# Reordering the head of a one-core decoder layer: x and its norm first, the modulation loads behind the w_in loads

## The chip, the cores and the metric

The kernel runs on one NeuronCore of a Trainium2 chip. The metric is the device time of one execution in microseconds (us), as the median of three runs. Matrix products run on the tensor engine (PE, with its weight loads as PEld), elementwise work on the vector engine (DVE), the scalar engine (ACT) and GpSimd (POOL). SyncE (SP) issues nearly all transfers from HBM; its queue and ACT's are shown as SPq and ACTq.

## The reference

One decoder layer on x (256 tokens, 1024 features). What matters here is how the first projection gets its input:

```python
c_act = jax.nn.silu(c)
mod = (c_act @ w_ada[l] + b_ada[l])[:, None, :]            # 1024 -> 6 x 1024
sh1, sc1, g1, sh2, sc2, g2 = jnp.split(mod, 6, axis=-1)
u = modulate(rmsnorm(h, norm1[l]), sh1, sc1)               # h = x; x_hat * (1 + sc1) + sh1
h = h + g1 * token_mixer(u, w_in[l], ...)                  # u @ w_in, retention, latent attention, w_out
u = modulate(rmsnorm(h, norm2[l]), sh2, sc2)
h = h + g2 * hier_moe(u, ...)                              # 32 experts, about 100 MB of weights
return rmsnorm(h, final_norm)
```

sh1 and sc1 need the first 2048 columns of w_ada (8 MB); every product u @ w_in needs them for its slice of features.

## The kernel before

All weights are streamed. SBUF is cut into 27 slots of 1 MB; a class `Loads` keeps a list of loads in a fixed order and issues each on SP's queue when a slot is free by a plan that a first pass over the program recorded. Accurate products are made of three: an operand is split into hi and lo parts (`split`: ACT writes hi at L463, DVE writes lo at L464), and hi x hi, lo x hi, hi x lo are summed (`mm3` at L378 to L380 for tokens on the partitions, `feat_mm` at L530 to L532 for features on the partitions).

The head of the kernel is a loop over k, eight slices of 128 features of u. For each slice it needs

- `ada` k: the 128 shift and 128 scale columns of w_ada for slice k, 1 MB, loaded as two transfers whose contiguous pieces are 128 columns (512 bytes). `ada_mm(k)` multiplies them with silu(c) on PE (L424) and DVE copies the sums out (L427). `mod_of(k)` turns them on PE (L440), and DVE makes the scale and shift columns `acl` and `shc` (L442 to L445).
- `x_turned(k)`: the normed x, turned by PE into a PSUM bank (L433).
- `u_of(k)`: ACT applies scale and shift from the PSUM bank (L449), ACT writes hi (L451), DVE lo (L452).
- `e0` k and `e1` k: the rows of w_in of slice k for 704 and for 512 columns (352 KB and 256 KB), split into three pieces. The two halves of `e0` feed twelve products of 352 columns (two groups of six, `n = 0, 1`), `e1` feeds twelve of 256 columns.

SP's order is ada 0, x, then for each k: ada k+1, e0 k, e1 k. After them come the other columns of w_in (the first is called rq1), rotary tables, and so on. PE's order in the loop is written out by hand: for 0 < k < 7 it is x_turned(k+1), ada_mm(k+1), the six products of n = 0, the turns of mod_of(k+1), the six of n = 1, then the twelve on `e1`. Until the first six products are issued the orders of DVE and ACT are written out as well; later a scheduler orders them. `keep_warm(n)` issues n products of ones on PE that no result uses (L387): nine at the start and eight after ada_mm(0).

In the start x arrives behind ada 0. ACT (L498) and DVE (L499) square it, POOL takes the power -1/2 (L368), ACT and DVE scale x (L511, L509), and PE turns the first slice.

Behind the last `u_of` ACT issues five small loads of its own (L1050 to L1054, router weights and biases); they are tied to come after the last L449. Then ACT copies the first finished sums out (L372) and splits rq1.

Of the kernel before, what the change touches and what calls it, by code (L numbers as in the profile page):

```python
# [9 lines left out]
F32 = mybir.dt.float32  # L10
# [3 lines left out]
AF = mybir.ActivationFunctionType  # L14
ALU = mybir.AluOpType
# [26 lines left out]
ATT_STEPS = ("s0",), ("s1",), ("t0",), ("o0", "t1", "s2"), ("o1", "s3"), ("t2",), ("o2", "t3"), ("o3",)  # L42
RET_STEPS = ("s0",), ("s1", "v0"), ("s2", "v1"), ("t0", "s3", "v2"), ("t1", "v3"), ("t2",), ("t3",)

WARM0 = 9, 8
WARM2 = 2
WARM3 = 1
WARM4 = 0
# [8 lines left out]
C_ID, C_IOTA, C_END = 0, 128, 160  # L57
# [147 lines left out]
def body(ctx, tc, A, out, plan=None):  # L205
    nc = tc.nc
    T, V, S, G, Q = nc.tensor, nc.vector, nc.scalar, nc.gpsimd, nc.sync
    st = ctx.enter_context(tc.tile_pool(name="st", bufs=1))
# [4 lines left out]
    LD = Loads(SL, plan)  # L213
    ring = Ring(SL)

    def bank(name="bank"):
        return PB.alloc(name)

    w_ada = A["w_ada"][0].rearrange("(k p) n -> p k n", p=128)
    w_in = A["w_in"][0].rearrange("(k p) n -> p k n", p=128)  # L220


    cst = st.tile([128, C_END], F32, name="cst")
    ev_s = SL.alloc("ev")
    csb = ev_s.t[:, 1024:1280].rearrange("p (k m) -> p k m", k=8)
    rows = ev_s.t[0:40, 1280:1408]
    x_s = SL.alloc("x")
    x = x_s.t.rearrange("p (b n) -> p b n", b=2)
# [8 lines left out]
    def ld_ada_early(k):  # L237
        def fn(t):
            v = t.rearrange("p (k s n) -> p k s n", k=8, s=2)
            for s in range(2):  # L240
                Q.dma_start(v[:, :, s, :], w_ada[:, :, s * 1024 + k * 128:s * 1024 + (k + 1) * 128])  # L241
        return fn

    def ld(view, src):
        def fn(t):
            n = 1
            for d in src.shape[1:]:
                n *= d
            Q.dma_start(t[:, :n].rearrange(view[0], **view[1]) if view else t[:, :n], src)  # L249
        return fn  # L250

    def ld_k(src):

        return ld(("p (k n) -> p k n", dict(k=src.shape[1])), src)


    LD.add(("ada", 0), ld_ada_early(0))
    LD.issue()
    for b in range(2):
        Q.dma_start(x[:, b, :], A["x"][0, b * 128:(b + 1) * 128, :])  # L260
    row_load(8, "norm1")
    row_load(16, "b_ada", 0, 2048)
    row_load(32, "q_norm")
    row_load(35, "kv_norm")
    for k in range(8):
        if k < 7:
            LD.add(("ada", k + 1), ld_ada_early(k + 1))
        LD.add(("e0", k), ld_k(w_in[:, k:k + 1, 4096:4800]))
        LD.add(("e1", k), ld_k(w_in[:, k:k + 1, 0:512]))
    uq = A["w_uq"][0].rearrange("(k p) n -> p k n", p=128)  # L270
    ukv = A["w_ukv"][0].rearrange("(k p) n -> p k n", p=128)
    def sq(name):
        return A[name][0].rearrange("(k p) n -> p k n", p=128)
# [5 lines left out]
    i = 0  # L279
    for name, c0 in (("rq1", 512), ("rk0", 1024), ("rk1", 1536), ("rv0", 2048), ("rv1", 2560), ("rg0", 3072), ("rg1", 3584),  # L280
                     ("gr0", 4800), ("gr1", 5312), ("gm0", 5824), ("gm1", 6336), ("w_mla_o", 0), ("w_mla_o", 512),
                     ("w_ret_o", 0), ("w_ret_o", 512)):
        for half in range(2):
            src = sq(name) if name in A else w_in
# [55 lines left out]
    ident = cst[:, C_ID:C_ID + 128]  # L340
# [15 lines left out]
    def small(n):  # L356
        if sml_n[0] + n > 256:
            sml_n[0] = 0
        a = sml[:, sml_n[0]:sml_n[0] + n]
        sml_n[0] += n  # L360
        return a
# [8 lines left out]
    def copy(eng, o, i):  # L370
        if eng is S:
            S.activation(o, i, AF.Copy)  # L372
        else:
            V.tensor_copy(o, i)
# [7 lines left out]
    def keep_warm(n, after=None):  # L382

        pb = bank()
        with tc.issue_after(after) if after is not None else ExitStack():
            for _ in range(n):
                T.matmul(pb.t, onesb, oneb[:, 0:1].to_broadcast([128, 512]), start=True, stop=True)  # L387
        pb.free()

    keep_warm(WARM0[0])  # L390

    u_s = SL.alloc("u")
    uf = u_s.t.rearrange("p (k t) -> p k t", k=8)
# [3 lines left out]
    xh = xh_s.t.rearrange("p (b n) -> p b n", b=2)  # L397
# [18 lines left out]
    shc = st.tile([128, 8], F32, name="shc")  # L416
    acl = st.tile([128, 8], F32, name="acl")

    def ada_mm(k, pa):

        ev = ev_s.t[:, 256 * (k % 2):256 * (k % 2 + 1)]
        t = LD.get(("ada", k)).t.rearrange("p (k n) -> p k n", k=8)
        for j in range(8):
            i = T.matmul(pa.t[32 * (j % 4):32 * (j % 4) + 32, :256], csb[:, j, :], t[:, j, :], start=j < 4, stop=j >= 4,  # L424
                         skip_group_check=True, tile_position=(0, 32 * (j % 4)))
        LD.done(("ada", k))
        V.tensor_copy(ev, pa.t[:, :256])  # L427
        return ev, i.ins

    def x_turned(k):  # L430
        px = bank()
        for b in range(2):
            T.transpose(px.t[:, b * 128:(b + 1) * 128], xh[:, b, k * 128:(k + 1) * 128], ident)  # L433
        return px

    last_u = [None]

    def mod_of(k, pa, ev):
        for i in range(2):
            T.transpose(pa.t[:, 256 + i * 128:256 + (i + 1) * 128], ev[:, i * 128:(i + 1) * 128], ident)  # L440
        sc = small(2)
        V.tensor_reduce(sc, pa.t[:, 256:512].rearrange("p (i j r) -> p i j r", i=2, j=4)[:, :, :, 0], AX.X, ALU.add)  # L442
        V.scalar_tensor_tensor(acl[:, k:k + 1], sc[:, 1:2], bsc1[:, k:k + 1], colt[:, 8 + k:9 + k], op0=ALU.add,
                               op1=ALU.mult)
        V.tensor_add(shc[:, k:k + 1], sc[:, 0:1], colt[:, 16 + k:17 + k])  # L445
        pa.free()

    def u_of(k, px):
        last_u[0] = S.activation(uf[:, k, :], px.t[:, 0:256], AF.Identity, bias=shc[:, k:k + 1], scale=acl[:, k:k + 1]).ins  # L449
        hi, lo = hi_lo("u", k)  # L450
        S.activation(hi, uf[:, k, :], AF.Copy)  # L451
        V.tensor_tensor(lo, uf[:, k, :], hi, ALU.subtract)  # L452
        px.free()

    u_blk = blk_of("u")

# [17 lines left out]
    colt = st.tile([128, 40], F32, name="colt")  # L474
    cs = st.tile([128, 8], F32, name="cs")
    G.memset(csb, 0.0)
    pb = bank()
    T.transpose(pb.t[:, :8], rows[:8, :], cst[:8, C_ID:C_ID + 8])
    th = small(8)
    S.activation(th, pb.t[:, 0:8], AF.Tanh, scale=0.5)  # L480
    V.tensor_scalar(th, th, 0.5, 0.5, op0=ALU.mult, op1=ALU.add)
    V.tensor_mul(cs, th, pb.t[:, 0:8])
    V.tensor_copy(csb[:, :, 0], cs)
    pb.free()
    pb = bank()
    T.transpose(pb.t[:, :37], rows[:37, :], cst[:37, C_ID:C_ID + 37])
    V.tensor_copy(colt[:, 8:37], pb.t[:, 8:37])
    pb.free()
    bsc1 = st.tile([128, 8], F32, name="bsc1")
    V.tensor_scalar(bsc1, colt[:, 24:32], 1.0, None, op0=ALU.add)  # L490
    pa0 = bank()
    ev0, i = ada_mm(0, pa0)
    keep_warm(WARM0[1])


    ss = small(4).rearrange("p (b h) -> p b h", b=2)
# [4 lines left out]
    rst = small(2)  # L501
    V.tensor_reduce(rst, ss, AX.X, ALU.add)
    rsqrt(rst, rst, 1.0 / D, EPS)
    mod_of(0, pa0, ev0)


    def scaled(b, c0, c1):
        if b:
            V.tensor_scalar(xh[:, 1, c0:c1], x[:, 1, c0:c1], rst[:, 1:2], None, op0=ALU.mult)  # L509
        else:  # L510
            S.activation(xh[:, 0, c0:c1], x[:, 0, c0:c1], AF.Copy, scale=rst[:, 0:1])  # L511

    scaled(0, 0, 128)
    scaled(1, 0, 128)
    scaled(0, 128, 384)
    scaled(1, 128, 1024)
    u_of(0, x_turned(0))
    hl0 = [split(early_w(0)[0], 352)]
    pa = bank()
    ev = ada_mm(1, pa)[0]  # L520
    keep_warm(WARM4)
    hl0.append(split(early_w(0)[1], 352))
    scaled(0, 384, 1024)
    def feat_mm(accs, hi, lo, mh, ml, k):

        for h in range(2):
# [9 lines left out]
    for k in range(8):  # L536
        hl = hl0 if k == 0 else []
        for w in early_w(k)[len(hl):]:
            hl.append(split(w, 352))
        LD.done(("e0", k))  # L540
        hl.append(split(LD.get(("e1", k)).t[:, :512].rearrange("p (k n) -> p k n", k=1), 512))
        LD.done(("e1", k))

        if 0 < k < 7:
            px, pa = x_turned(k + 1), bank()
            ev = ada_mm(k + 1, pa)[0]
        for n in range(2):
            s, hi, lo = hl[n]
            for b in range(2):
                mm3(eacc[n][b].t[:, :352], u_blk(k, b), (hi[:, 0, :], lo[:, 0, :]), k == 0, k == 7)  # L550
            s.free()
            if (n, k) == (0, 0):
                start.close()
                early = ExitStack()
                early.enter_context(tc.manual_schedule(engines={T.engine}))
                px = x_turned(1)
            if n == (k == 0) and k < 7:
                mod_of(k + 1, pa, ev)
                u_of(k + 1, px)
        if k == 0:  # L560
            eacc.append([bank("acc") for _ in range(2)])
        s, hi, lo = hl[2]
        feat_mm(eacc[2], hi[:, 0, :], lo[:, 0, :], *hi_lo("u", k), k)
        s.free()
    early.close()
    LD.margin = MARGIN[1]
    u_s.free()
# [981 lines left out]
    with tc.If(many > CAP):  # L1549
# [7 lines left out]
        for k2 in range(4):  # L1557
            pb = bank()
# [3 lines left out]
            for kk in range(2):  # L1562
                k = 2 * k2 + kk
                S.activation(u2[:, k, :], pb.t[:, kk * 256:(kk + 1) * 256], AF.Identity, bias=s2c[:, k:k + 1],
                             scale=a2c[:, k:k + 1])
# [4 lines left out]
        with tc.For_i(0, 32, 1) as e:  # L1570
            for n in ("w1", "w3", "w2"):
                src = A[n][0].rearrange("g i (p k) n -> (g i) p k n", p=128)
# [12 lines left out]
            for b in range(2):  # L1585
                for n in range(2):
                    pb = bank()
# [124 lines left out]
```

## Time and profile before

| | us |
|---|---|
| median of 3 runs (lowest to highest) | 521.34 (520.93 to 521.62) |
| the profiled execution | 521.56 |
| its span, first to last instruction | 519.8 |
| PE busy in the span | 492.7 (95%) |
| DVE, ACT, POOL busy | 286.4, 197.9, 56.8 |
| HBM read, mean rate over the span | 173.22 MB, 335 GB/s |

Times in the views are counted from the start of the span. Busy time of PE is modelled from its issue and says little of how dense it is; what releases an instruction, and when, is read from the views of waits and of instructions in order of time.

### The profile page before, as it was taken

The page shows a single profiled execution, that of the slowest core. Times are in us where ns is not written, and L with a number is a line of the kernel's source. Part 1 is how long each engine was busy: PE and PEld are TensorE (multiplying, and loading weights), DVE is VectorE, ACT ScalarE, POOL GpSimd, SP SyncE. Part 2 cuts the span into 40 slices and gives each one's busy share as a digit, 9 for nine tenths or more (in the row PEclk, how much of TensorE's full clock was granted, in tenths as well). Part 3 has the DMA queues.
Part 4 walks back from the last instruction along what each step waited for, and adds up shares of the span by engine and source line. Part 5 has one row for each costly group of instructions (what it writes and reads, how often), then busy time and mean ns, then how long its engine had stood idle before and what let it go on. Part 6 is the DMA issues. An engine that isn't in the chain of part 4 may idle for free.

```text
span 519.8 us, 8582 instructions
## 1 busy us (share of the span) xinstructions
PE 492.7 (95%) x3440; PEld 339.1 (65%) x3443; DVE 286.4 (55%) x525; ACT 197.9 (38%) x366; POOL 56.8 (11%) x50
## 2 busy tenths in 40 slices
PE   6899999999999999999999999999999989898994
PEld 2678999997887878888688887443344343434432
DVE  3455789884696987979966746414031313131213
ACT  3545773454677544557434424202020211121013
POOL 1000321411000001119800000000000000000000
PEclk9999999999999999999999999999999999999999
DMA  9999899788876782998689888999999999999992
GB/s 272 323 320 361 297 353 398 289 321 312 333 242 244 247 321 81 338 396 308 234 342 352 311 352 301 417 386 422 420 417 419 421 415 419 421 419 416 392 325 99
DMA packets 68097, 174.85 MB, mean 336 GB/s; under 512 B 5422, under 2 KB 27091, under 8 KB 57816
## 3 DMA queue, kind: packets, MB, share of 16 engines
q1 hardware_dynamic: 65602, 174.01, 89.8%
q10 hardware_dynamic: 2454, 0.27, 0.4%
q8 instruction: 28, 0.46, 0.4%
q14 instruction: 13, 0.11, 0.1%
HBM read 173.22 MB, written 1.05 MB: 335 GB/s over the span
## 4 chain that ended last, share of the span: by engine, by line
PE 74%; DVE 8%; DMA 6%; SPq 5%; ACT 3%; issue 2%; POOL 1%; ACTq 1%; DVEq 0%; POOLq 0%
PE b L1403 11%; PE b L378 8%; PE b L380 8%; PE b L379 8%; PE b L1514 6%; PE b L1523 5%; PE b L1343 5%; SPq L249 3%; DVE s L464 3%; DMA s<-in_w_in 2%; SPq L241 2%; DMA s<-in_w 2%; PE b L1354 1%; PE b L1543 1%; ACT s L463 1%
## 5 line engine op out<-in xcount | busy, mean ns | idle before, releaser
L464 DVE TENSOR_TENSOR s<-s,s 128x1024 fp32r<-128x1024 f32 (+2 forms) x92 | 110.9, 1219 | 41.5 <-ACT s L463 40.5
L463 ACT ACTIVATE s<-s 128x1024 fp32r<-128x1024 f32 (+2 forms) x92 | 83.3, 922 | 86.9 <-PE b L380 53.7
L378 PE MATMUL b<-s,s 128*128 128x512 f32 (+2 forms) x258 | 102.2, 396 | 1.3 <-ACT s L463 1.3
L380 PE MATMUL b<-s,s 128*128 128x512 f32 (+2 forms) x258 | 99.4, 385 | 1.3 <-DVE s L464 1.3
L379 PE MATMUL b<-s,s 128*128 128x512 f32 (+2 forms) x258 | 98.1, 380 | 0.0
L1403 PE MATMUL b<-s,s 128*32 128x256 f32 x1024 | 61.4, 380 | 0.0
L378 PEld LDWEIGHTS b<-s,s 128*128 128x128 f32 x258 | 48.5, 188 | 15.6 <-ACT s L463 4.4
L380 PEld LDWEIGHTS b<-s,s 128*128 128x128 f32 x258 | 48.4, 188 | 13.2 <-DVE s L464 3.8
L379 PEld LDWEIGHTS b<-s,s 128*128 128x128 f32 x258 | 48.5, 188 | 8.5 <-issue 0.2
L1403 PEld LDWEIGHTS b<-s,s 128*32 128x32 f32 x1024 | 32.8, 110 | 31.1 <-issue 9.9
L1061 DVE SCALAR_TENSOR_TENSOR s<-s,cs,s 128x1024 f32<-128x1024 f32 x32 | 41.4, 1293 | 0.3
L532 PE MATMUL b<-s,s 128*128 128x256 f32 x128 | 36.2, 284 | 0.5 <-DVE s L464 0.5
L530 PE MATMUL b<-s,s 128*128 128x256 f32 x128 | 36.4, 285 | 0.0
L531 PE MATMUL b<-s,s 128*128 128x256 f32 x128 | 36.1, 283 | 0.0
L1495 ACT ACTIVATE wr<-b 128x256 f32<-128x256 f32 x8 | 3.1, 383 | 78.5 <-PE b L1403 73.7
L1514 PE MATMUL b<-s,wr 128*32 128x512 f32 x224 | 32.8, 596 | 0.0
L1343 PE MATMUL b<-s,sml 128*128 128x512 f32 x56 | 26.9, 603 | 5.3 <-DVE sml L1339 5.3
L1337 DVE TENSOR_TENSOR S<-cst,rk 128x128 f32<-128x128 f32 x16 | 4.1, 287 | 48.9 <-PE b L1457 48.9
L1130 POOL TENSOR_TENSOR s<-s,s 128x1024 f32<-128x1024 f32 x8 | 25.8, 3260 | 13.0 <-DVE s L464 13.0
L1523 PE MATMUL b<-s,rt 128*128 128x512 f32 x56 | 26.2, 611 | 0.0
L372 ACT ACTIVATE s<-b 128x512 f32<-128x512 f32 (+2 forms) x25 | 14.1, 568 | 31.0 <-PE b L1343 12.5
L532 PEld LDWEIGHTS b<-s,s 128*128 128x128 f32 x128 | 24.4, 191 | 0.9 <-DVE s L464 0.9
(258 smaller groups left out, 654.7 us busy)
## 6 DMA issues: line engine op xcount, KB each, us to landing
s<-in_w SPq DMA_DIRECT2D x92, 1024.0 KB
s<-in_w_in SPq DMA_DIRECT2D x22, 1024.0 KB
s<-in_w_ada SPq DMA_DIRECT2D x16, 1024.0 KB
s<-in_w_ada SPq DMA_DIRECT2D x16, 512.0 KB
s<-in_w_mla_o SPq DMA_DIRECT2D x4, 1024.0 KB
s<-in_w_ret_o SPq DMA_DIRECT2D x4, 1024.0 KB
s<-in_w_out SPq DMA_DIRECT2D x4, 1024.0 KB
s<-in_w SPq DMA_DIRECT2D x6, 512.0 KB
```

Of the source, the lines that this page charges most:

```text
L378: T.matmul(o, l[0], r[0], start=start, stop=False, skip_group_check=True)
L379: T.matmul(o, l[1], r[0], start=False, stop=False, skip_group_check=True)
L380: return T.matmul(o, l[0], r[1], start=False, stop=stop, skip_group_check=True)
L463: S.activation(hi, src, AF.Copy)
L464: V.tensor_tensor(lo, src, hi, ALU.subtract)
L530: T.matmul(o, hi[:, f], mh, start=k == 0 and c == 0, stop=False, skip_group_check=True)
L532: T.matmul(o, lo[:, f], mh, start=False, stop=k == 7, skip_group_check=True)
L1061: V.scalar_tensor_tensor(a, t[:, kk, :], cs[:, k:k + 1], a, op0=ALU.mult, op1=ALU.add)
L1343: T.matmul(pg[k4].t, Sr[:, b], hp[:, b, 4 * k4:4 * k4 + 4, :].rearrange("p k q -> p (k q)"), start=b == 0, stop=b == 1, skip_group_check=True)
L1403: i = T.matmul(ph.t[32 * j:32 * j + 32, m * 256:(m + 1) * 256], ug[:, k, 32 * j:32 * j + 32], w, start=k == 0, stop=k == 7, skip_group_che ...
L1514: T.matmul(py[n].t[32 * j:32 * j + 32, :], hdT[:, k, 32 * j:32 * j + 32], ts[j][:, k, n * 512:(n + 1) * 512], start=k == 0, stop=k == 1, s ...
L1523: T.matmul(fin[2 * b + n].t, GT[:, b * 128:(b + 1) * 128], y[:, n * 512:(n + 1) * 512], start=bt == 0, stop=bt == 7, skip_group_check=True)
```

## The change

SP issues x ahead of ada 0, and for each k `e0` k and `e1` k ahead of ada k+1. The squares of x and its inverse root stand ahead of the silu of c. All of x is scaled in one place, and x is turned two slices at a time: slices 0 and 1 from one PSUM bank ahead of ada_mm(0), 2 and 3 right behind it, 4 and 5 behind the products of k = 1, 6 and 7 behind those of k = 2. Except for slice 0 they are copied to `uf` in SBUF, and `u_of` works there in place. ada_mm(k+1) moves from ahead of the products of slice k to behind its first six, and mod_of(k+1) with u_of(k+1) from behind those six to behind the second six. The second keep_warm has 4 products in place of 8.

```diff
-WARM0 = 9, 8
+WARM0 = 9, 4
...
+    for b in range(2):
+        Q.dma_start(x[:, b, :], A["x"][0, b * 128:(b + 1) * 128, :])
     LD.add(("ada", 0), ld_ada_early(0))
     LD.issue()
-    for b in range(2):
-        Q.dma_start(x[:, b, :], A["x"][0, b * 128:(b + 1) * 128, :])
...
     for k in range(8):
+        LD.add(("e0", k), ld_k(w_in[:, k:k + 1, 4096:4800]))
+        LD.add(("e1", k), ld_k(w_in[:, k:k + 1, 0:512]))
         if k < 7:
             LD.add(("ada", k + 1), ld_ada_early(k + 1))
-        LD.add(("e0", k), ld_k(w_in[:, k:k + 1, 4096:4800]))
-        LD.add(("e1", k), ld_k(w_in[:, k:k + 1, 0:512]))
...
-    def x_turned(k):
+    def x_turned(i):
+
         px = bank()
-        for b in range(2):
-            T.transpose(px.t[:, b * 128:(b + 1) * 128], xh[:, b, k * 128:(k + 1) * 128], ident)
+        for kk in range(2):
+            for b in range(2):
+                T.transpose(px.t[:, (2 * kk + b) * 128:(2 * kk + b + 1) * 128],
+                            xh[:, b, (2 * i + kk) * 128:(2 * i + kk + 1) * 128], ident)
         return px
...
-    def u_of(k, px):
-        last_u[0] = S.activation(uf[:, k, :], px.t[:, 0:256], AF.Identity, bias=shc[:, k:k + 1], scale=acl[:, k:k + 1]).ins
+    def u_of(k, src=None):
+        last_u[0] = S.activation(uf[:, k, :], uf[:, k, :] if src is None else src, AF.Identity, bias=shc[:, k:k + 1],
+                                 scale=acl[:, k:k + 1]).ins
...
     V.tensor_copy(csb[:, :, 0], cs)
     pb.free()
+    keep_warm(WARM0[1])
...
+    def turned(i, eng):
+        px = x_turned(i)
+        copy(eng, uf[:, 2 * i:2 * i + 2, :], px.t.rearrange("p (k t) -> p k t", k=2))
+        px.free()
+
+    for c0, c1 in ((0, 256), (256, 1024)):
+        for b in range(2):
+            scaled(b, c0, c1)
...
+    px0 = x_turned(0)
     pa0 = bank()
     ev0, i = ada_mm(0, pa0)
...
+    turned(1, S)
     mod_of(0, pa0, ev0)
...
+    u_of(0, px0.t[:, 0:256])
     hl0 = [split(early_w(0)[0], 352)]
-    pa = bank()
-    ev = ada_mm(1, pa)[0]
-    keep_warm(WARM4)
+    V.tensor_copy(uf[:, 1, :], px0.t[:, 256:512])
+    px0.free()
     hl0.append(split(early_w(0)[1], 352))
...
-        if 0 < k < 7:
-            px, pa = x_turned(k + 1), bank()
-            ev = ada_mm(k + 1, pa)[0]
         for n in range(2):
...
-            if n == (k == 0) and k < 7:
+            if k < 7 and n == 0:
+                pa = bank()
+                ev = ada_mm(k + 1, pa)[0]
+            elif k < 7:
                 mod_of(k + 1, pa, ev)
-                u_of(k + 1, px)
+                u_of(k + 1)
...
+        if k in (1, 2):
+            turned(k + 1, (S, V)[k - 1])
```

## Rows read from the trace of the kernel before

**Rows 1.** Chain that ended last, 0 to 75 us: start, length, what held it.
```profile
33.66 7.45 DMA s<-in_w_in
...
49.55 0.57 ACT s L449
...
50.83 1.88 ACTq L1052
```

**Rows 2.** Stretches: us, busy PE, PEld, DVE, ACT, POOL, granted clock, DMA share, GB/s.
```profile
9.50:11.50 2.00, 1.03 (x6) 0.48 (x4) 1.40 (x9) 0.61 (x2) 0.70 (x1) 1.00 1.21 293
35.00:40.00 5.00, 5.00 (x44) 3.92 (x44) 2.46 (x9) 2.44 (x5) 0.00 (x0) 1.00 1.15 318
47.00:50.00 3.00, 3.00 (x23) 2.74 (x20) 3.00 (x10) 2.56 (x6) 0.96 (x1) 1.00 1.04 386
395.00:400.00 5.00, 5.00 (x100) 2.99 (x92) 0.00 (x0) 0.00 (x0) 0.00 (x0) 1.00 1.02 421
```

**Rows 3.** DMA issues to 50 us by size: queue, count, KB each.
```profile
s<-in_w_ada SPq DMA_DIRECT2D x16, 512.0 KB
s<-in_w_in SPq DMA_DIRECT2D x8, 352.0 KB
s<-in_w_in SPq DMA_DIRECT2D x8, 256.0 KB
```

**Rows 4.** ACT in order of time: start, length, [idle before <- what ended it].
```profile
44.12 0.56 ACT L449 ACTIVATE s<-b,shc,acl 128x256 f32<-128x256 f32 x1 [1.23 <-DVE shc L445]
44.71 0.42 ACT L451 ACTIVATE s<-s 128x256 fp32r<-128x256 f32 x1
46.30 1.40 ACT L463 ACTIVATE s<-s 128x352 fp32r<-128x352 f32 x3 [1.17 <-DMA s<-in_w_in]
47.94 1.41 ACT L463 ACTIVATE s<-s 128x352 fp32r<-128x352 f32 x3 [0.24 <-DMA s<-in_w_in]
...
49.57 0.37 ACTq L1050 DMA_DIRECT2D n2c<-in_norm  x1
...
52.81 0.46 ACT L372 ACTIVATE s<-b 128x352 f32<-128x352 f32 x1 [2.24 <-DMA s<-in_w_in]
```

**Rows 5.** PE in order of time, the last steps of the loop and behind it.
```profile
43.02 0.44 PE L440 MATMUL b<-cst,s 128*128 128x128 f32 x2
...
46.00 1.07 PE L424 MATMUL b<-s,s 128*32 128x256 f32 x16
47.00 0.43 PE L378 MATMUL b<-s,s 128*128 128x352 f32 x1
...
48.37 0.41 PE L378 MATMUL b<-s,s 128*128 128x352 f32 x1
...
49.41 0.28 PE L530 MATMUL b<-s,s 128*128 128x256 f32 x1
...
50.85 0.32 PE L378 MATMUL b<-s,s 128*128 128x352 f32 x1
...
55.53 0.39 PE L532 MATMUL b<-s,s 128*128 128x256 f32 x1 [0.52 <-DVE s L464]
```

**Rows 6.** All engines in order of time, 0 to 20 us.
```profile
1.00 4.02 PE L387 MATMUL b<-oneb 128*128 128x512 bf16 x9 [1.00 <-POOL mhalf L352]
...
8.39 1.92 PE L387 MATMUL b<-oneb 128*128 128x512 bf16 x8
...
9.39 0.63 ACT L498 ACTIVATE s<-s 128x512 f32<-128x512 f32 x1 [0.61 <-DMA s<-in_x]
...
11.99 0.84 PE L433 MATMUL b<-cst,s 128*128 128x128 f32 x4 [1.45 <-ACT s L511]
...
14.44 0.42 PE L378 MATMUL b<-s,s 128*128 128x352 f32 x1 [0.27 <-ACT s L463]
```

**Rows 7.** DVE in order of time, around the last mod_of.
```profile
48.04 0.68 DVE L464 TENSOR_TENSOR s<-s,s 128x512 fp32r<-128x512 f32 x1
48.65 0.17 DVE L442 TENSOR_REDUCE sml<-b 128x2 f32<-128x8 f32 x1
```

More of the change, by code (lines that the diff above doesn't have):

```diff
@@ L452, in u_of @@
         V.tensor_tensor(lo, uf[:, k, :], hi, ALU.subtract)
-        px.free()
     u_blk = blk_of("u")
@@ L476, in body @@
     G.memset(csb, 0.0)
+    ss = small(4).rearrange("p (b h) -> p b h", b=2)
+    for b in range(2):
+        S.activation(xh[:, b, 0:512], x[:, b, 0:512], AF.Square, accum_out=ss[:, b, 0:1])
+        V.scalar_tensor_tensor(xh[:, b, 512:1024], x[:, b, 512:1024], 1.0, x[:, b, 512:1024], op0=ALU.mult, op1=ALU.mult,
+                               accum_out=ss[:, b, 1:2])
+    rst = small(2)
+    V.tensor_reduce(rst, ss, AX.X, ALU.add)
+    rsqrt(rst, rst, 1.0 / D, EPS)
     pb = bank()
@@ L484, in body, with scaled @@
     pb.free()
+    keep_warm(WARM0[1])
+    def scaled(b, c0, c1):
+        if b:
+            V.tensor_scalar(xh[:, 1, c0:c1], x[:, 1, c0:c1], rst[:, 1:2], None, op0=ALU.mult)
+        else:
+            S.activation(xh[:, 0, c0:c1], x[:, 0, c0:c1], AF.Copy, scale=rst[:, 0:1])
+    def turned(i, eng):
[3 more added lines that the diff above has]
+    for c0, c1 in ((0, 256), (256, 1024)):
+        for b in range(2):
+            scaled(b, c0, c1)
     pb = bank()
@@ L490, in body @@
     V.tensor_scalar(bsc1, colt[:, 24:32], 1.0, None, op0=ALU.add)
+    px0 = x_turned(0)
     pa0 = bank()
     ev0, i = ada_mm(0, pa0)
-    keep_warm(WARM0[1])
-    ss = small(4).rearrange("p (b h) -> p b h", b=2)
-    for b in range(2):
-        S.activation(xh[:, b, 0:512], x[:, b, 0:512], AF.Square, accum_out=ss[:, b, 0:1])
-        V.scalar_tensor_tensor(xh[:, b, 512:1024], x[:, b, 512:1024], 1.0, x[:, b, 512:1024], op0=ALU.mult, op1=ALU.mult,
-                               accum_out=ss[:, b, 1:2])
-    rst = small(2)
-    V.tensor_reduce(rst, ss, AX.X, ALU.add)
-    rsqrt(rst, rst, 1.0 / D, EPS)
-    mod_of(0, pa0, ev0)
[L507 to L517, printed above, removed]
+    turned(1, S)
+    mod_of(0, pa0, ev0)
+    u_of(0, px0.t[:, 0:256])
     hl0 = [split(early_w(0)[0], 352)]
-    pa = bank()
-    ev = ada_mm(1, pa)[0]
-    keep_warm(WARM4)
+    V.tensor_copy(uf[:, 1, :], px0.t[:, 256:512])
+    px0.free()
     hl0.append(split(early_w(0)[1], 352))
-    scaled(0, 384, 1024)
     def feat_mm(accs, hi, lo, mh, ml, k):
@@ L555, in body @@
                 early.enter_context(tc.manual_schedule(engines={T.engine}))
-                px = x_turned(1)
-            if n == (k == 0) and k < 7:
+            if k < 7 and n == 0:
+                pa = bank()
+                ev = ada_mm(k + 1, pa)[0]
+            elif k < 7:
                 mod_of(k + 1, pa, ev)
-                u_of(k + 1, px)
+                u_of(k + 1)
         if k == 0:
```

## The prediction

> **What bounds the kernel now.** I read the chain of waits first. Up to 47.7 us it consists almost wholly of SP's queue and of transfers of w_ada and w_in; then it passes through the last u_of on ACT (L449 at 49.55), ACT's own small loads (L1052, 1.88 us), and from there to ACT's copy and the split of rq1 [rows 1, 4]. So the head is bound by the stream of weights, and the change must be measured against that stream.
>
> Then the stretches. While only w_ada moves, the DMA share is 1.21 at 293 GB/s; where rows of 2 KB move, 386 GB/s; over a whole step 318 GB/s [rows 2]. The queues are full, and the rate hangs on what is moved, not on when it is asked for. A step moves 2 x 512 + 352 + 256 = 1632 KB [rows 3], or 1.671 MB; at 318 GB/s that is 5.25 us. One ada (1.049 MB at 293 GB/s) is 3.58 us of it.
>
> The third view is PE in order of time. From 47.00 to 50.85 it has no gap: six products, two turns and six products more (to 49.41), twelve products (to 50.85) [rows 5]. With 1.0 us for ada_mm (46.00 to 47.00) and some 0.3 us for turning x, a step of PE is about 5.2 us too. The stream and PE run level, with PE some tenths behind.
>
> What follows the head carries a shift on. Up to about 300 us PE works without long gaps and loads wait for slots that it frees; in the expert part the stream is full (421 GB/s, share 1.02 [rows 2]), and its loads wait for slots that PE has left. I therefore count a shift at 55 us one for one at the end.
>
> **The change, part by part.**
>
> *x ahead of ada 0.* The bytes ahead of the first modulation are the same: x and ada 0. ada 0 now lands when the second half of x did, at 9.39 [rows 6]. x lands 3.58 us earlier (the price of ada 0), at about 5.8. In the kernel before, 3.44 us passed from the second half of x to the end of its first turns (9.39 to 12.83) [rows 6]; the same work now ends at about 9.3. It is needed at u_of(0) near 11.9, so 2.6 us cover it. Tanh of c now stands behind the squares of x on ACT, and ada_mm(0) needs it. By those times the squares end near 6.6, against ada 0 at 9.39: hidden, and on the path only if c or x were 2.5 us later.
>
> From ada 0: ada_mm 1.0, copy 0.4 (an estimate from the 0.42 us that ACT takes for 256 columns [rows 4]), turns to the start of u 1.1 (43.02 to 44.12 [rows 4, 5]), u 0.56, hi 0.42 [rows 4], the first piece of w_in 0.45 (a third of 1.41 [rows 4]). The sum is 13.3 us. It was 14.44 [rows 6]: a lead of 1.1 us at the first product.
>
> *w_in ahead of the next ada.* e0 k and e1 k come 3.58 us earlier, ada k+1 comes 608 KB later. ada 7 takes the place in the stream that e1 6 had. e0 6 landed at 46.30 and e0 7 at 47.94 [rows 4]; between them lie e1 6 (256 KB) and e0 7 (352 KB), so e1 6 landed at about 46.30 + 1.64 x 256 / 608 = 46.99. The change takes no byte out of the stream ahead of ada 7, so ada 7 lands there however early the loop began.
>
> *ada_mm and mod_of behind the products.* After its landing the last modulation has to pass ada_mm (1.0), the second six products (48.37 to 49.41: 1.04 [rows 5]), and from the first turn to the start of u 1.1: 46.99 + 3.14 = 50.13, against 49.55 before [rows 1]. This is 0.58 us late. u and hi take 0.98 more and hand-offs 0.1: slice 7 starts on PE at 51.2, against 50.85 [rows 5], 0.35 late. If u, now read from SBUF, takes 0.42 as L451 does in place of 0.56, it is 0.2 late. Every earlier step obeys the same sum: six products, 1.0, 1.04, 1.1, 0.98 and 0.1 make 5.2 us, as much as the stream takes. The loop can keep its lead of 1.1 us up to slice 6 and loses it at slice 7, where the kernel before had only twelve and twelve products left and nothing to wait for.
>
> *Turns two slices at a time.* PE makes as many as before. Those for slices 4 to 7 follow the products of k = 1 and 2, when PE waits for hi anyway (1.44 us of products on e1 against 2.1 us from the turns to hi). ACT gains two copies of 512 columns and DVE one, each about as long as L451 with twice the columns (at most 0.84 us), and DVE one of 256. They fall in the first 30 us, where the lead covers them; without it each would cost at most its length once. Four warm products fewer are 0.96 us of an idle PE (1.92 for eight [rows 6]): nothing, while the clock holds.
>
> *Behind the head.* ACT's loads are tied to the last L449. If L1052 holds ACT for 1.88 us from its issue on, L372 and the split of rq1 come 0.58 later. If it holds until the full queue takes it, which depends on the stream alone, they come no later. L1050, the same kind of transfer with less to it, took 0.37 [rows 4], so most of the 1.88 is waiting and I take half of 0.58, 0.3 us. PE's own 0.35 goes into the 0.52 us for which it waits for DVE at 55.53 [rows 5]. The stream as a whole I leave where it was (bounds: 0.3 us earlier, if x ahead of ada 0 starts it better; nothing later).
>
> The sum: 521.56, the profiled execution's own time, + 0.3 = 521.86. That execution lies 0.22 over the median, so the forecast for the median is 521.6 us. Bounds of the unknown parts: from -0.3 (stream earlier, hold with the stream) to +0.6 (hold with u) make 521.0 to 521.9.
>
> **A rule that speaks against it.** The nine products of ones at the start take 0.45 us each, the eight later ones of the same shape 0.24 [rows 6]: 1.2 GHz in the first stretch, 2.4 GHz in the second; the granted clock then stays at 1.00 [rows 2]. The Trainium skill, page "TensorE: Matmul & The Clock Gate", section "Part 1: The HAM clock gate", says that the throttled clock is the default and that only activity releases it. By that rule the halved keep_warm and the wait ahead of slice 0 could put PE back to 1.2 GHz, and the sum would be that of the third rival. By the rows, nearly 2 us of idle PE behind the first nine products did not hinder full speed at 8.39.
>
> **The rivals.**
>
> *Faster: the lead survives.* For it: ACT's hold behind L1052 is on the chain, and a loop that runs 1.1 us ahead up to slice 6 could pull it in if ada 7 lands earlier than I interpolated, or if the scheduler, which orders ACT and DVE anew, shortens what stands between u and the split of rq1. Against: the stream is full and its bytes are the same. It decides if ada 7 lands by 45.9. Price: -1.1, at most about -1.5 with the hold gone: 520.2 us.
>
> *Slower: the scheduler puts the splits of w_in k+1 behind u_of(k+1) on ACT.* Then slice k+1 waits for hi of u and after it for a piece of w_in (0.45 on ACT, 0.5 on DVE): a step takes 5.7 in place of 5.2 us. Seven such steps cost 3.5 us, less the lead of 1.1: +2.4, or 523.7 us. For it: the program now has u_of(k+1) ahead of those splits. Against: at the end of the loop before, the splits of slice 7 (47.94) ran ahead of the last u (49.55) although the program has them behind [rows 1, 4]; ACT takes what is ready.
>
> *Slower, milder: DVE makes lo of e1 ahead of the columns of mod_of.* It did so at 48.04, and the sums began only at 48.65 [rows 7]. In the new order e1 lands just ahead of those sums; 0.68 us [rows 7] once at the last step, on top of the 0.58, makes 0.3 + 0.7 = +1.0 to +1.3: 522.5 us. In this case I also count the clock: at half speed the first steps lose some 2 us, 1.1 of it out of the lead, and the rest comes back only slowly: +0.9, or 522.2 us.
>
> *The change does not do what it says:* ada 0 lands as late as x did, so the first product hardly moves. That would spend the lead at once, and the end is the forecast's.
>
> **How the numbers follow.** A difference under 0.2%, 1.04 us, can't be told from no change here. The forecast (521.6, its own range 521.0 to 521.9, the silent start included) gets 0.52 and counts as no change; the faster rival 0.20; the order on ACT 0.13; DVE's order and the clock 0.15, both taken as slower. So faster 0.20, same 0.52, slower 0.28. The range reaches down to the faster rival and up past the milder slower ones; it leaves out the order on ACT and the ends, not quite 2 in 10: 520.1 to 523.0 us.
>
> **What would show it.** In the changed profile the first L378 near 13.3 in place of 14.44 (right, if x is turned when ada 0 lands). L424 of each step should wait for w_ada, the last one starting at 47.0; then the last L449 near 50.1 and slice 7 on PE near 51.2. If L424 runs behind PE's own work without waiting, the step is PE's, not the stream's. If the wait of PE in the loop is for L463, it is the order on ACT; if L442 starts late behind L464, that on DVE. L372 near 53.1 is half the hold; at 52.8 the hold is the queue's. The prediction is wrong if slice 7 starts by 50.3, if the order of loads behind the head changes and moves a stall of the middle part, or if the shift at 55 us is not found again at the end.

## The result and the profile after

| us | median | lowest to highest | ratio to before, 95% |
|---|---|---|---|
| before, beside it | 521.48 | 520.93 to 522.17 (4 runs) | |
| after | 526.29 | 524.37 to 528.12 (4 runs) | 1.0090 [1.0066, 1.0115] |

The change makes the kernel 0.9% slower. The forecast was no change, and its range ended at 523.0. Three single executions in this study stand far outside all others (571, 629 and 1309 us) and are left out of every comparison.

The profiled execution of after took 524.37 us (span 522.3), the lowest of its four times: its trace holds 2.8 of the slowdown, and some 2 us of the median have to be looked for in another execution (after run once more, below). The lines have moved: the products on tokens are still L378 to L380, `ada_mm` L424; the turns of `mod_of` are L443, its columns L445 to L448; `u_of` is L452 (u), L455 (hi), L456 (lo); `split` is L466 and L467; the products on features are L537 to L539.

The start, all engines in order of time, answers to [rows 6] (start, length, [idle before <- what ended it]):

```profile
0.82 0.86 SPq L258 DMA_DIRECT2D s<-in_x  x2
...
2.69 2.04 SPq L241 DMA_DIRECT2D s<-in_w_ada  x2
...
5.76 0.63 ACT L484 ACTIVATE s<-s 128x512 f32<-128x512 f32 x1 [0.54 <-DMA s<-in_x]
...
6.22 1.89 PE L387 MATMUL b<-oneb 128*128 128x512 bf16 x4
...
10.37 1.07 PE L424 MATMUL b<-s,s 128*32 128x256 f32 x16 [0.87 <-DMA s<-in_w_ada]
...
14.43 0.43 PE L378 MATMUL b<-s,s 128*128 128x352 f32 x1 [2.01 <-ACT s L466]
```

The second half of x starts its squares at 5.76 (forecast: about 5.8), and x is turned by 9.5. But ada 0 arrives at 10.3, not at 9.39, and the first product starts at 14.43, where it stood before (14.44 in [rows 6]). There is no lead.

What PE waited for up to 60 us, summed by line (us in total, times, longest):

```profile
PE b L378 <- ACT s L466: 2.0, 1, 2.0
PE b L378 <- ACT s L455: 1.5, 4, 0.8
PE b L537 <- ACT s L466: 1.1, 1, 1.1
...
PE b L424 <- DMA s<-in_w_ada: 0.9, 1, 0.9
```

PE waits for w_ada once in the whole head, for ada 0. The loop waits for ACT instead. One step of it, PE, ACT and DVE in order of time, answers to [rows 4, 5]:

```profile
27.57 1.07 PE L424 MATMUL b<-s,s 128*32 128x256 f32 x16
28.57 0.43 PE L378 MATMUL b<-s,s 128*128 128x352 f32 x1
...
29.64 0.38 PE L443 MATMUL b<-cst,s 128*128 128x128 f32 x2
...
30.39 0.15 DVE L448 TENSOR_TENSOR shc<-sml,colt 128x1 f32<-128x1 f32 x1
...
30.58 0.60 ACT L452 ACTIVATE s<-s,shc,acl 128x256 f32<-128x256 f32 x1 [1.24 <-DVE shc L448]
...
31.21 0.42 ACT L455 ACTIVATE s<-s 128x256 fp32r<-128x256 f32 x1
...
31.66 0.42 DVE L456 TENSOR_TENSOR s<-s,s 128x256 fp32r<-128x256 f32 x1 [1.12 <-ACT s L455]
31.68 0.43 PE L378 MATMUL b<-s,s 128*128 128x352 f32 x1
...
32.14 0.19 PEld L379 LDWEIGHTS b<-s,s 128*128 128x128 f32 x1 [0.27 <-DVE s L456]
32.14 0.43 PE L379 MATMUL b<-s,s 128*128 128x352 f32 x1
...
33.15 1.07 PE L424 MATMUL b<-s,s 128*32 128x256 f32 x16
```

This is a closed chain: from each start to the next, ada_mm 1.00, six products 1.07, turns to the start of u 0.94, u 0.63, hi 0.47, six products 1.47, and ada_mm again, with nothing between them. The sum is 5.58 us. The last six products take 0.4 us longer than the others because the second of them (L379) needs lo of u, which DVE finishes at 32.08. The eight starts of L424 are 10.37, 15.83, 21.98, 27.57, 33.15, 38.71, 44.30 and 49.87; from the third on they are 5.56 to 5.59 us apart, with no wait for a transfer. Before, the last three steps took 5.14 to 5.25 us, the longest 6.46 (23.95 to 30.41), and the last start stood at 46.00 [rows 5]. The one longer step after, 15.83 to 21.98, has 0.6 us of DVE's lo of `e1` between the two parts of `mod_of`:

```profile
18.32 0.17 DVE L445 TENSOR_REDUCE sml<-b 128x2 f32<-128x8 f32 x1
18.49 0.69 DVE L467 TENSOR_TENSOR s<-s,s 128x512 fp32r<-128x512 f32 x1
19.10 0.21 DVE L446 SCALAR_TENSOR_TENSOR acl<-sml,bsc,colt 128x1 f32<-128x1 f32 x1
```

The end of the head, ACT and then PE in order of time, answers to the ends of [rows 4, 5]:

```profile
52.90 0.60 ACT L452 ACTIVATE s<-s,shc,acl 128x256 f32<-128x256 f32 x1 [3.24 <-DVE shc L448]
53.79 1.06 ACT L466 ACTIVATE s<-s 128x1024 fp32r<-128x1024 f32 x1 [0.29 <-PE b L539]
...
54.75 0.40 ACT L455 ACTIVATE s<-s 128x256 fp32r<-128x256 f32 x1
...
55.36 0.33 PE L378 MATMUL b<-s,s 128*128 128x352 f32 x1
```

ACT takes a split of rq1 (L466, 1024 columns) between the last u and its hi. From the start of u to the first product of slice 7 that makes 2.46 us, against 1.10 in the step above. Slice 7 starts at 55.36, 4.5 us after its place in [rows 5]. From the first product of slice 0 to that of slice 7 there are seven steps: before 36.41 us (14.44 to 50.85), 5.20 a step; after 40.93 (14.43 to 55.36). Seven times 0.38 for the chain (2.7), 0.5 more in the step of slice 1 and 1.4 for the split of rq1 make the difference.

The shift goes on to the end. One line of the expert part in both traces, after and then before (duration min/median/max, first and last start):

```profile
L1411 PE MATMUL b<-s,s x1024: 379/379/404, 324.7 to 502.4; 128*32 128x256 f32 x171
```
```profile
L1403 PE MATMUL b<-s,s x1024: 379/379/404, 321.4 to 499.0; 128*32 128x256 f32 x171
```

It is 3.3 us at 321 us and 3.4 at 499. Of the 4.5 us 3.8 are left at 56 us and 3.4 at 100 us (start of the same PE instruction in both traces). In the tail a wait of 0.5 us for the last weights, which before had at L1622, is gone. 2.8 us are left in the time of the execution, 2.5 in its span.

### The profile page after: what moved, and what is told of

Same layout as the page of the kernel before. It is cut to its first block, busy times and chain, and to the rows that moved or that the text cites. A ratio compares the mean times of both kernels' runs of the same rounds, so it can differ in the third digit from the quotient of the medians.

```text
span 522.3 us, 8580 instructions
## 1 busy us (share of the span) xinstructions
PE 494.9 (95%) x3439; PEld 339.7 (65%) x3439; DVE 287.8 (55%) x527; ACT 199.4 (38%) x367; POOL 58.5 (11%) x50
## 3 DMA queue, kind: packets, MB, share of 16 engines
HBM read 173.22 MB, written 1.05 MB: 334 GB/s over the span
## 5 line engine op out<-in xcount | busy, mean ns | idle before, releaser
L467 DVE TENSOR_TENSOR s<-s,s 128x1024 fp32r<-128x1024 f32 (+2 forms) x92 | 110.6, 1213 | 41.0 <-ACT s L466 40.7
L466 ACT ACTIVATE s<-s 128x1024 fp32r<-128x1024 f32 (+2 forms) x92 | 84.3, 924 | 88.6 <-PE b L380 55.0
L378 PE MATMUL b<-s,s 128*128 128x512 f32 (+2 forms) x258 | 102.5, 397 | 3.6 <-ACT s L466 2.0
L380 PE MATMUL b<-s,s 128*128 128x512 f32 (+2 forms) x258 | 98.9, 383 | 1.0 <-DVE s L467 0.9
L379 PE MATMUL b<-s,s 128*128 128x512 f32 (+2 forms) x258 | 98.7, 382 | 0.2
L378 PEld LDWEIGHTS b<-s,s 128*128 128x128 f32 x258 | 48.5, 188 | 18.8 <-issue 4.9
L380 PEld LDWEIGHTS b<-s,s 128*128 128x128 f32 x258 | 48.4, 188 | 11.9 <-DVE s L467 3.0
L379 PEld LDWEIGHTS b<-s,s 128*128 128x128 f32 x258 | 48.5, 188 | 10.1 <-DVE s L456 1.6
L537 PE MATMUL b<-s,s 128*128 128x256 f32 x128 | 37.0, 289 | 1.1 <-ACT s L466 1.1
L539 PE MATMUL b<-s,s 128*128 128x256 f32 x128 | 35.9, 283 | 0.4 <-DVE s L467 0.4
L372 ACT ACTIVATE s<-b 128x512 f32<-128x512 f32 (+2 forms) x27 | 15.3, 570 | 34.2 <-PE b L1351 12.5
L537 PEld LDWEIGHTS b<-s,s 128*128 128x128 f32 x128 | 24.4, 191 | 1.4 <-ACT s L466 1.3
```

What stands on the lines that cost most here:

```text
L378: T.matmul(o, l[0], r[0], start=start, stop=False, skip_group_check=True)
L379: T.matmul(o, l[1], r[0], start=False, stop=False, skip_group_check=True)
L380: return T.matmul(o, l[0], r[1], start=False, stop=stop, skip_group_check=True)
L466: S.activation(hi, src, AF.Copy)
L467: V.tensor_tensor(lo, src, hi, ALU.subtract)
L537: T.matmul(o, hi[:, f], mh, start=k == 0 and c == 0, stop=False, skip_group_check=True)
```

## The experiments

Theory, formed from these rows: the new place of ada_mm and mod_of makes the loop a chain that no longer fits under the stream, and the slow clock of PE, where it occurs, adds to a chain and not to a wait. Rivals: the new order of loads delays the modulations; the four warm products left out are the whole cost. Medians are compared with runs of before on the same chip (521.53 for the first four kernels, 521.36 for the next four, 521.27 for the last four).

**The order on PE put back** (the order of loads, x first and four warm products stay):

```diff
+    pa = bank()
+    ev = ada_mm(1, pa)[0]
...
+        if 0 < k < 7:
+            pa = bank()
+            ev = ada_mm(k + 1, pa)[0]
...
-            if k < 7 and n == 0:
-                pa = bank()
-                ev = ada_mm(k + 1, pa)[0]
-            elif k < 7:
+            if n == (k == 0) and k < 7:
```

> PE's order in the loop put back (ada_mm ahead of the products of a step, mod_of behind the first six); the order of the loads, x first and the four warm products stay as changed. Order theory (the new order closes a chain of dependences of 5.58 us a step, where the stream needs 5.2): the step goes back to about 5.2 us, ada 7 lands near 47 and is waited for, slice 7 starts near 52 in place of 55.4, and the time is 522 to 523 us. Loads theory (ada behind w_in is what costs): PE now waits for each ada, the time stays at 524 us or more. Clock theory (fewer warm products cost the rest): the runs still spread over 3 us or more.

Measured: 522.16 us, ratio 1.0025 [1.0014, 1.0036]. Four of the five us are gone. PE in order of time, the last ada_mm, and the window of 10 to 15 us (us, busy PE, PEld, DVE, ACT, POOL, granted clock, DMA share, GB/s):

```profile
46.93 1.07 PE L424 MATMUL b<-s,s 128*32 128x256 f32 x16
```
```profile
10.00:15.00 5.00, 3.29 (x22) 1.67 (x21) 0.98 (x5) 1.71 (x4) 0.00 (x0) 0.50 1.16 319
```

With the old order of PE the last ada_mm runs at 46.93 and does not wait, so ada 7 had landed by the time that the prediction worked out (46.99): the bytes of the new load order were counted rightly. PE had only half its clock here for a stretch of about 10 us, and the last ada_mm still stands only 0.9 us behind its place in [rows 5]. Slice 7, however, starts at 53.38, not near 52: DVE's lo of `e1` stands between the two parts of the last `mod_of`, and ACT takes rq1's split (51.81) ahead of the last hi (52.77), as in after. Against the kernel before, the same PE instructions start 1.9 us later at 56 us and 1.1 us later at 100 us.

**The order of loads put back** (the new order on PE stays):

```diff
-        LD.add(("e0", k), ld_k(w_in[:, k:k + 1, 4096:4800]))
-        LD.add(("e1", k), ld_k(w_in[:, k:k + 1, 0:512]))
         if k < 7:
             LD.add(("ada", k + 1), ld_ada_early(k + 1))
+        LD.add(("e0", k), ld_k(w_in[:, k:k + 1, 4096:4800]))
+        LD.add(("e1", k), ld_k(w_in[:, k:k + 1, 0:512]))
```

> Only the order of the loads put back: ada k+1 ahead of the w_in rows of slice k, as before. Order theory: the chain of 5.58 us a step stays, no step waits for ada, the time stays within 1 us of the changed kernel (525 to 527 us). Loads theory: 521 to 522.5 us.

Measured: 531.92 us, ratio 1.0206 [1.0191, 1.0220], worse than after by 5.6 us and far from what either theory expected. ACT in one step, in order of time, and the product that waits for it:

```profile
36.22 0.50 ACT L466 ACTIVATE s<-s 128x352 fp32r<-128x352 f32 x1 [3.50 <-DMA s<-in_w_in]
36.63 0.59 ACT L452 ACTIVATE s<-s,shc,acl 128x256 f32<-128x256 f32 x1
37.12 0.48 ACT L466 ACTIVATE s<-s 128x352 fp32r<-128x352 f32 x1
37.50 0.40 ACT L455 ACTIVATE s<-s 128x256 fp32r<-128x256 f32 x1
```
```profile
37.96 0.42 PE L378 MATMUL b<-s,s 128*128 128x352 f32 x1 [0.62 <-ACT s L455]
```

Now the rows of w_in arrive when u is due, and ACT splits them ahead of u and between u and hi. The chain grows to 5.9 to 6.3 us a step. That is close to the prediction's second rival, u and the splits of w_in in each other's way on ACT: it shows not in the changed kernel, but in that kernel without its order of loads. The new load order is therefore not what makes the slowdown; under the new order of PE it saves 5.6 us.

**Both put back** (left of the change: x and its norm first, turns in twos, four warm products): the edits of the two above.

> Both orders put back; what is left of the change is x ahead of ada 0, its norm ahead of the silu of c, the turns two slices at a time and four warm products in place of eight. Order theory: 521 to 522 us, as before. Start theory (x first costs): the first product is no earlier than 14.4 us, and the time is 1 us or more over the kernel before. Clock theory: a wide spread and a mean granted clock under 0.995 in some runs.

Measured: 520.88 us, ratio 0.9992 [0.9983, 1.0002]. The rest of the change costs nothing and brings nothing that can be told. The slowdown lies in the order on PE and what it does to the loop. The order of loads alone is not free, though: under PE's old order the new one costs 1.3 us (522.16 against 520.88). Without it slice 7 starts at 50.83 as before, with it at 53.38; which part of the 1.3 us that is was not tested.

**Eight warm products again** in after:

```diff
-WARM0 = 9, 4
+WARM0 = 9, 8
```

> The changed kernel with eight warm products in the second place, as before. Clock theory: the runs draw together to within 1.5 us and the median falls by about 2 us, to the 524 us of the fastest run of the changed kernel. Order theory alone: no change beyond 0.5 us, 525.5 to 526.5 us, spread as before.

Measured: 526.08 us, ratio 1.0089 [1.0073, 1.0105], no gain, though the runs lie within 0.7 us. But the clock was not held either: the first ada_mm ran at full speed (1.07 us), the second, behind PE's wait of 2 us ahead of the first product, did not (1.94); the granted clock is 0.66 in the window of 15 to 20 us, and one step took 7.65 us. Eight products in this place do not bring the time back; whether the clock costs it, this run could not tell.

**After once more, and after kept warm.** The second has eight warm products and seven more in PE's wait ahead of the first product:

```diff
-WARM0 = 9, 4
+WARM0 = 9, 8
...
     mod_of(0, pa0, ev0)
+    keep_warm(7)
```

> The changed kernel once more, beside the next three on the same chip: 526.3 us by its first four runs. Clock theory: its runs spread over 3 us again (524 to 528), the later ones with a lower mean granted clock. Order theory alone: they lie within 1.5 us of one another.

> The changed kernel with eight warm products in the second place and seven more behind the first mod_of, where PE stands idle for 2 us ahead of the first product. Clock theory: PE stays at full speed through the head, the runs lie within 1 us of one another, and the median is 524.3 us, that of the fastest run of the changed kernel: 2 us under it. Order theory: the step stays at 5.58 us and 3 us over the kernel before remain, so not under 524 us. If the median is 526 us the clock is not what spreads the runs.

Measured: 527.03 us, ratio 1.0116 [1.0101, 1.0131], and 524.69 us, ratio 1.0068 [1.0055, 1.0081]. The spread of over 3 us did not come again in the first: its four runs lie within 1.28 us, all with a mean granted clock of 0.985 or 0.986. The window of 10 to 15 us of the first, then of the second:

```profile
10.00:15.00 5.00, 3.41 (x22) 1.84 (x22) 0.88 (x4) 1.26 (x3) 0.00 (x0) 0.50 1.15 320
```
```profile
10.00:15.00 5.00, 4.34 (x32) 2.29 (x33) 2.06 (x8) 2.35 (x5) 0.00 (x0) 1.00 1.15 317
```

PE in the first: the four warm products, then a wait for ada 0, behind which ada_mm is slow.

```profile
6.17 1.05 PE L387 MATMUL b<-oneb 128*128 128x512 bf16 x4
...
10.33 1.94 PE L424 MATMUL b<-s,s 128*32 128x256 f32 x16 [1.20 <-DMA s<-in_w_ada]
```

At 1.2 GHz the first ada_mm of the first takes 1.94 us, the first product starts at 15.75 in place of 14.23, and L424 of slice 3 stands at 30.09 against 27.37: 2.7 us, which stay. Kept warm, all runs lie within 0.28 us (524.63 to 524.91), as against 526.59 to 527.87. So the clock costs 2.3 us of this median of after (527.03 - 524.69), and 3.3 us are left without it. That it also makes the spread of the first four runs is likely but not shown: 524.37 us had a mean clock of 0.996 and 528.12 one of 0.985, but 526.75 one of 0.995.

**ada_mm at the top of the step** (the order of PE before, except that mod_of and u stay behind the second six products):

```diff
+        if 0 < k < 7:
+            pa = bank()
+            ev = ada_mm(k + 1, pa)[0]
...
-            if k < 7 and n == 0:
-                pa = bank()
-                ev = ada_mm(k + 1, pa)[0]
-            elif k < 7:
+            if n == 1 and k < 7:
```

> ada_mm(k+1) back at the top of a step, mod_of and u_of(k+1) left behind the second six products, all else as changed. Chain theory (it is ada_mm inside the way from one hi to the next that makes the step 5.58 us): the step falls to the stream's 5.2 us, PE waits for ada 7 near 47.0 and slice 7 starts near 52.3, the time is 522.5 to 523.5 us. Rival (the late mod_of is what costs): the step stays over 5.5 us and the time within 1 us of the changed kernel.

Measured: 523.25 us, ratio 1.0043 [1.0030, 1.0056]. PE, the last ada_mm:

```profile
47.25 1.07 PE L424 MATMUL b<-s,s 128*32 128x256 f32 x16 [0.34 <-DMA s<-in_w_ada]
```

It waits for its transfer again, as four others of the eight do (5.3 us in all), and stands at 47.25 in place of 49.87. Here ada_mm goes ahead of the first six products, which wait for hi, so it no longer stands between them and the next turns. Its place in the chain is what made the loop longer than the stream. The five executions follow the mean clock: 522.07 us at 0.998, 523.03 at 0.993, 523.25 at 0.991, 523.65 at 0.985, 523.94 at 0.981. So a slow clock goes with up to 1.9 us here too, although the loop waits for the stream; and in the one execution near full clock ada_mm's place brings 2.6 us against after kept warm (524.69), with 0.7 left over before. rq1's split stands ahead of the last hi here as well (52.13 against 53.09).

**Hi of the last u ahead of rq1's splits**, in after:

```diff
-        S.activation(hi, uf[:, k, :], AF.Copy)
+        last_hi[0] = S.activation(hi, uf[:, k, :], AF.Copy).ins
...
-        r = split(t[:, 2 * kp:2 * kp + 2, :], w)
+        with tc.issue_after(last_hi[0]):
+            r = split(t[:, 2 * kp:2 * kp + 2, :], w)
```

> The changed kernel with ACT's split of rq1 held behind the last hi of u (in the changed kernel ACT takes the split first, 1.06 us, and slice 7 waits for hi). If that order costs what it seems to: slice 7 starts 0.9 us earlier and the time falls by 0.7 to 1.2 us against the changed kernel. If PE only swaps work (it takes products on rq1 while it waits): no difference beyond 0.4 us.

Measured: 525.86 us, ratio 1.0076 [1.0055, 1.0096]: 1.2 us less than after beside it (527.03). ACT in order of time:

```profile
56.36 0.60 ACT L452 ACTIVATE s<-s,shc,acl 128x256 f32<-128x256 f32 x1 [3.21 <-DVE shc L448]
...
56.99 0.42 ACT L455 ACTIVATE s<-s 128x256 fp32r<-128x256 f32 x1
57.32 2.00 ACT L466 ACTIVATE s<-s 128x1024 fp32r<-128x1024 f32 x2
```

Slice 7 starts on PE at 57.47, 1.1 us after u began, in place of 2.46. (All times of this execution stand later because its first ada_mm began at 11.34, 1 us later than in after, and its first two ran at the low clock.) One of its six executions, with a mean clock of 0.998, took 522.52 us; the other five took 525.54 to 526.46.

**Kept warm and hi first together**, to see whether the parts add up; the edits of both:

> The changed kernel with the two repairs together that leave its orders alone: PE kept at full speed (worth 2.3 us alone) and rq1's split behind the last hi (worth 1.2 us alone). If the parts add up: 524.7 less 1.2, 523.2 to 523.8 us, with a spread under 1 us; the 2 us that remain over the kernel before are the longer step (seven times 0.38 us, less what it gains elsewhere).

Measured: 523.13 us, ratio 1.0034 [1.0023, 1.0046]. They add up: 3.33 us over before for the kept-warm kernel become 1.86 us. The step is still 5.58 us, the last L424 at 50.17. The 1.9 us left are put down to the longer loop, with the longer step of slice 1 in it. The runs spread over 1.9 us, not under 1, with mean clocks of 0.994 to 0.998: what spreads them is open.

**The best without the new order on PE: both put back and kept warm**, and the same with ACT's five small loads behind the last u moved to SP:

```diff
-WARM0 = 9, 4
+WARM0 = 9, 8
...
+    keep_warm(4)
```
```diff
-        with tc.issue_after(last_u[0]):
-            S.dma_start(cols2, A["norm2"][0].rearrange("(p k) -> p k", k=8))
...
+        Q.dma_start(cols2, A["norm2"][0].rearrange("(p k) -> p k", k=8))
...
```

> Both orders put back, x and its norm first, PE kept at full speed through the head (eight warm products in the second place, four behind the first mod_of). If the loop of the kernel before has cover for a slow clock: no change against the same kernel with four warm products (520.9 us), 520.3 to 521.2 us. If the clock costs it as much as the changed kernel: 1 us or more faster, under 520 us.

> The same, and the five small router loads issued on SP's queue in place of ACT's, where they stand between the last u and the split of rq1. If ACT's hold of 1.88 us behind them is on the path: 0.5 to 1.1 us faster than the kernel it is made from, 519.5 to 520.3 us. If the stream sets when rq1 can be split: no difference beyond 0.4 us.

Measured: 520.84 us, ratio 0.9990 [0.9982, 0.9999], and 520.34 us, ratio 0.9985 [0.9975, 0.9994]. Holding the clock brings nothing over the kernel with both put back (0.9992), whose clock fell in its profiled execution (0.76 in 10 to 15 us): its loop hides a slow clock. The second is the best of the study, faster than before by 0.9 us, less than the 0.2% at which a difference can be told from none in single medians. The 0.5 us that ACT's own loads seem to be worth (520.84 - 520.34) lie at the edge of both expectations and under what can be told: whether ACT's hold was on the path stays open.

**Before without its eight second warm products**:

```diff
-WARM0 = 9, 8
+WARM0 = 9, 0
```

> The kernel before with no warm products in the second place. Clock theory as a matter of the place alone: PE falls to half speed in the head here too and the time rises by 2 us. Cover theory (its loop waits for the stream, and slow products hide in that wait): the granted clock falls below 1.00 between 10 and 20 us, and the time stays within 0.7 us of the kernel before.

Measured: 520.56 us, ratio 0.9986 [0.9977, 0.9995]. The window of 10 to 15 us:

```profile
10.00:15.00 5.00, 2.89 (x20) 1.29 (x20) 2.72 (x11) 2.56 (x7) 0.74 (x1) 0.50 1.15 323
```

The clock is halved as in after once more, and the time is no longer, 0.7 us shorter if anything; the four executions with a mean clock under 0.990 took 520.21 to 520.60 us, the other eight 520.15 to 521.33. The loop of before has waits in which a slow PE catches up: ada_mm of slice 2 starts at 19.51, against 18.77 in the kernel before, that of slice 4 at 30.33, against 30.41, and the last at 45.92, against 46.00 [rows 5].

## Why the prediction was wrong

**Right: what bounds the head before, and the bytes.** The order of loads takes nothing out of the stream ahead of ada 7: with ada_mm at the top of the step the last one waited for it until 47.25, and with PE's order put back it ran at 46.93 without waiting; forecast 46.99. x and its norm are hidden behind ada 0. A shift at the end of the head reaches the end of the kernel: 3.8 us at 56 us, 3.3 in the expert part, 2.8 at the end.

**The step that failed: "Every earlier step obeys the same sum: six products, 1.0, 1.04, 1.1, 0.98 and 0.1 make 5.2 us, as much as the stream takes."** The chain was the right one, and one of its terms was mis-sized. The first six products measured 1.47 us, not 1.0, because the second of them waits for lo of u, which the sum left out: lo follows hi on DVE (0.42 us), while only the first product can start on hi. The 1.0 was read from [rows 5], where ada_mm (46.00 to 47.00) stood between hi and these products, so that lo was done at 45.59, before they began:

```profile
45.16 0.43 DVE L452 TENSOR_TENSOR s<-s,s 128x256 fp32r<-128x256 f32 x1 [1.14 <-ACT s L451]
```

Moving ada_mm behind the products took that cover away. In before the chain is also shorter, without ada_mm and the other six between u and the next u, and the stream leaves it room. The other terms nearly cancel: turns to u 0.94 in place of 1.1, u from SBUF 0.60 where 0.56 was taken (0.42 was hoped for). At 5.2 us chain and stream would have been level; at 5.58 the chain is the bound, and each of seven steps adds 0.38 us to the 5.20 that a step took before: the last ada_mm, forecast at 47.0, ran at 49.87, and slice 7, forecast at 51.2, started at 55.36. No run took away the wait for lo alone; that it is the missing 0.4 us is read from the trace. The prediction had the question in its list ("if L424 runs behind PE's own work without waiting, the step is PE's"), and the answer is that one, with the addition that it was not PE's work but a chain through PE, DVE and ACT.

**The lead of 1.1 us did not come.** The sum from ada 0 to the first product held (forecast 3.9, measured 4.06); ada 0 came 0.9 us late. The prediction took it that with the same bytes ahead it would land when x did. The rate from 5 to 6 us was low, after and then before:

```profile
5.00:6.00 1.00, 0.03 (x1) 0.00 (x0) 0.29 (x3) 0.46 (x3) 0.00 (x0) 1.00 0.93 266
```
```profile
5.00:6.00 1.00, 0.27 (x2) 0.18 (x1) 0.34 (x2) 0.18 (x1) 0.00 (x0) 1.00 1.26 306
```

But over the whole start it was not lower: 270 GB/s up to 10.37 us, where ada 0 was there, and before 258 up to 9.39, where x was. That is 2.80 MB against 2.42, of which x and ada 0 are 2.10 in both. So some 0.4 MB more of other loads had moved by then, an estimated 1.2 us at 318 GB/s: the bytes ahead were not the same, because loads issued behind ada 0 moved beside it. This is the rival "does not do what it says". It was said to leave the end at the forecast's, and it did no harm of its own in the kernel with both parts put back (520.88), where ada 0 was also waited for until 10.0.

**"Four warm products fewer [...]: nothing, while the clock holds."** The clock did not hold in most executions (its mean over the span is 0.990 or less in six of the eight of after, 0.994 to 0.997 in the five of after kept warm), and the 2.3 us that it cost are more than the third rival's 0.9. That price took a loss of some 2 us and let the lead of 1.1 cover most of it. There was no lead, and a chain that has no wait in it gave nothing back. The kernel before without its second warm products does give it back (0.50 in 10 to 15 us, no time lost), and so does the kernel with both orders put back (520.57 to 521.32 us in the executions with a mean clock of 0.990 to 0.992, 520.13 to 521.39 in the others). The rule of the Trainium skill, page "TensorE: Matmul & The Clock Gate", section "Part 1: The HAM clock gate", that the throttled clock is the default and activity releases it, spoke against the change here. The traces agree in the direction: 1.2 GHz behind the waits for ada 0 and ahead of the first product (granted 0.50), 2.4 GHz where eight products of ones stood ahead of the first wait and seven in the second (1.00). But the profiled execution of after had the same wait of 2.01 us ahead of the first product and kept 1.00 behind it.

**Not foreseen: rq1's split ahead of the last hi.** Because the head ended later, rq1 was there when the last u was, and ACT, which takes what is ready, split it first. It cost 1.2 us (525.86 against 527.03) and, kept warm, 1.5 (3.33 against 1.86 over before, on two chips). The prediction used the same readiness of ACT to argue that the splits of w_in would run ahead of u; it did not ask what else would be ready by then.

**DVE's order** (the lo of `e1` ahead of the columns of mod_of) happened once in after, in the modulation of slice 1, for 0.6 us, and not at the last step, where the rival had it; it is at the last step in the kernel with only PE's order put back. **ACT's hold** behind its own loads was no bound: the load that took 1.88 us in [rows 1] took 0.55 here, behind the products that mattered.

The sum, in medians: after is 5.7 us over before on the chip of the second four kernels (527.03 against 521.36); of that 2.3 is the clock, 1.2 to 1.5 rq1's split, and the remaining 1.9 to 2.1 the longer loop. At slice 7 the longer steps (2.7) and the one of slice 1 (0.5) come to 3.2; the shift shrinks from 4.5 us there to 2.8 at the end, and how the loss is shared between the parts was not followed.

## What to carry to other kernels

Before an instruction that waits for a transfer is moved behind other work, write down the closed chain from one of its starts to the next, through every engine and with the second operand of each product (lo as well as hi), and compare it with what the stream takes: being level is no margin. A loop with enough wait for a stream can hide a slow clock and a late operand; one whose chain is the bound pays for both in full. So the second set of warm-up products was worth nothing in the kernel before, and eleven more of them were worth 2.3 us in the changed one. How much wait is enough has to be measured: with ada_mm alone put back the loop waits for the stream five times, and its time still rose as the clock fell. Where a scheduler hands an engine what is ready first, a later critical operation meets work that was not yet there before, and has to be put ahead by hand.

## What the runs showed of the hardware

- The granted clock of TensorE fell to 0.50 in the head in several kernels and executions (0.50 in the window of 10 to 15 us of three kernels shown above), and not in others of the same kernel: the profiled execution of after had 1.00 in every window from 10 us on. After spread over 3.8 us in its first four runs and 1.3 in the next four, over 0.28 in five kept warm; but the kernel with both repairs, kept warm too, spread over 1.9 us in eight.
- The four warm products of that profiled execution took 0.47 us each (1.89 for four), those of the same kernel's other profile 0.26 (1.05 for four); the one with the slow products kept the full clock afterwards, and the other lost it by its first ada_mm (1.94 us).
- The same activation of 256 columns took 0.60 us from SBUF (L452 in the loop) and 0.56 from PSUM (L449 in [rows 4], and L452 for slice 0): copying the turned x to SBUF gained nothing there.
- x ahead of ada 0 made ada 0 land 0.9 us later than x had in the other order, at no lower mean rate (270 against 258 GB/s): 2.80 MB had moved by then as against 2.42, 2.10 of them x and ada 0. Loads issued later on the same queue had moved beside the earlier ones. Which order of the start would avoid it was not tested.
